# Stick-breaking attention in a hybrid decoder block: differences of V in place of the second sigmoid, the product and the triangular selection

## The chip, the cores and the metric

The kernel runs on one core of a Trainium2 chip. Its time is the device time of one execution in microseconds; smaller is better. The core has five engines that run side by side, each with its own queue of instructions worked off in order: PE (matrix products and transposes), DVE (vector), ACT (scalar, activations), POOL (GpSimd) and SP, which here only issues transfers. Engines wait for each other by semaphores. SBUF is the working memory with 128 partitions, PSUM the small memory into which PE writes.

## The reference

One decoder layer on 1040 tokens (16 learned ones and 1024 real ones) of width 1024. The part that matters here is attention with 16 heads of width 64:

```python
# A[t,s] = sigmoid(z_ts) * prod_{s<j<t} (1 - sigmoid(z_tj)), s < t
z = jnp.einsum("bqhd,bkhd->bhqk", qb, kb) * scale
causal = s_idx < t_idx
log_beta = jax.nn.log_sigmoid(z)
log_fail = jnp.where(causal, log_beta - z, 0.0)
survive = lax.cumsum(log_fail, axis=3, reverse=True) - log_fail
a = jnp.where(causal, jnp.exp(log_beta + survive), 0.0)
o = jnp.einsum("bhqk,bkhd->bqhd", a, vb)
```

Beside attention stand a gated short convolution on the same normalised input, two gates, an output projection, and a gated feed-forward part with a second convolution. Everything is float32; the kernel splits each operand of a large product into a high and a low part and makes two or three products of them.

## The kernel before, in words

The first 940 us are one mixed stage. PE works through a list of 128-column blocks of the input projection (`items`, lines 400 to 416): for each pair of heads p the items of V, Q and K, three of the convolution, and one to four gates. Each item has three chunks of 342 columns and in each chunk eight steps of three products (lines 129 to 131, tile `mm`). Between these steps attention is woven in, unit by unit. A unit is one head and one third of the queries, that is three blocks of 114 queries (`QB`).

- `stage1` (line 316) makes, for each block of queries and each chunk of keys, the products z (lines 330, 331), and on ACT sigmoid(-z) into `fl` (line 332) and sigmoid(z) into `be` (line 333). A deferred step `weights` then runs on DVE a scan over the keys from right to left (line 340). It multiplies up `fl` and takes the maximum with `upper`, which is 1 in the triangle at and above the diagonal, so that the running product starts at 1 there. POOL multiplies `be` by the scan shifted by one key (line 346, in pieces) and zeroes the triangle (line 348). `be` is then A.
- `stage2` (line 358) transposes A in blocks of keys on PE (line 377, tile `tp`), ACT and DVE split it into `ah` and `al` (`split`, lines 65 and 66), and PE multiplies by V (lines 367, 368). ACT and DVE gather the result in `ot` (lines 394, 395), and after the last unit of a pair SP writes `ot` to `o_d`.
- `item_v` (line 246) copies V from PSUM into `vt` with ACT (line 253), transposes it in nine blocks of keys on PE (line 263) in three deferred steps, and splits it into `vv`.

All the weights come in by SP, are cast to a high part by ACT (line 110, `whi`) and subtracted by POOL (line 113, `wlo`), two items ahead.

At the start, nine blocks of input rows (`xt`) are loaded, squared and summed by ACT (line 460), scaled by DVE after a square root on ACT (lines 73 to 78, 462, tile `xn`), transposed by PE (line 184) and split into `xnT`. The first products need the first three blocks.

The order in which the instructions are written is not the order in which each engine has them: a scheduler goes through them with its own estimates of durations, picks for each engine what is ready by those, and gives out the buffers of the pools (a `tag` names a set of slots, `bufs` their number). `ps_tp`, the PSUM tiles `tp` for all transposes of this stage, has two. `fl` has two buffers and `be` six; the `xt` blocks of the start use the tag `be` and the `xn` blocks the tag `fl`. The tag `wk` has four, shared by `vt`, the tiles of the convolution, the gates and `ot`.

Of the kernel before, what the change touches and what calls it, by code (L numbers as in the profile page):

```python
# [8 lines left out]
F32 = mybir.dt.float32  # L9
F32R = mybir.dt.float32r  # L10
AF = mybir.ActivationFunctionType
ALU = mybir.AluOpType
# [21 lines left out]
def block_kernel(ctx, tc, x, meta_tokens, g_pre_mix, w_in, channels, w_proj_conv,  # L34
# [177 lines left out]
    CH_C = [(T0 - 2, CH + 2), (T0 + CH, CH), (T0 + 2 * CH, CH)]  # L212
    CH_K = [(0, T0 + CH), (T0 + CH, CH), (T0 + 2 * CH, CH)]

    QH, QL, KK, V = {}, {}, {}, {}

    def item_q(p):
        def evac(ci, a, n, ps):
# [27 lines left out]
    def item_v(p):  # L246
        st = {}

        def evac(ci, a, n, ps):
            if ci == 0:  # L250
                st["vt"] = work.tile([P, NT], F32, name="vt", tag="wk", bufs=4)
            vt = st["vt"]
            nc.scalar.copy(vt[:, a:a + n], ps)
            if ci < 2:
                return
            vv = heads.tile([P, 9, 2, P], F32R, name="vv", tag="vv", bufs=2)
            V[p] = vv

            def tokens(k0, kn, m):
                tp = ps_tp.tile([P, 512], F32, name="tp", tag="tp")  # L260
                for k in range(kn):
                    s0 = KEYS[k0 + k][0]
                    nc.tensor.transpose(tp[:m, k * P:(k + 1) * P], vt[:, s0:s0 + m], ident)
                tv = tp[:m, :kn * P].rearrange("p (k h d) -> p k h d", k=kn, h=2)
                split(vv[:m, k0:k0 + kn, :, 0:64], vv[:m, k0:k0 + kn, :, 64:128], tv)

            dense.defer(1, lambda: tokens(0, 4, P))
            dense.defer(2, lambda: tokens(4, 4, P))
            dense.defer(3, lambda: tokens(8, 1, QB))
        return (col_block(w_in, 40 + p), src_x, CH_K, evac)  # L270
# [45 lines left out]
    def stage1(p, h, g):  # L316
        res = []
        qh, ql, kk = QH[p][h], QL[p][h], KK[p][h]
        for b in range(3 * g, 3 * g + 3):
            nk = P + QB * b  # L320
            q0 = QB * b
            fl = work.tile([P, NT], F32, name="fl", tag="fl")[:QB]
            be = work.tile([P, NT], F32, name="be", tag="be", bufs=6)[:QB]
            nch = -(-nk // 512)
            wch = 2 * (-(-nk // (2 * nch)))
            c0 = 0
            while c0 < nk:
                n = min(wch, nk - c0)
                z = ps_z.tile([P, 512], F32, name="z", tag="z")[:QB, :n]
                nc.tensor.matmul(z, qh[:, q0:q0 + QB], kk[:, c0:c0 + n], start=True, stop=False)  # L330
                nc.tensor.matmul(z, ql[:, q0:q0 + QB], kk[:, c0:c0 + n], start=False, stop=True)  # L331
                nc.scalar.activation(fl[:, c0:c0 + n], z, AF.Sigmoid, scale=-0.125)  # L332
                nc.scalar.activation(be[:, c0:c0 + n], z, AF.Sigmoid, scale=0.125)
                c0 += n
                if late:
                    late.pop(0)()
                if c0 < nk:
                    yield n
            def weights(fl=fl, be=be, nk=nk):
                nc.vector.tensor_tensor_scan(fl[:, :nk][:, ::-1], fl[:, :nk][:, ::-1],  # L340
                                             upper[:, NT - nk:][:, ::-1], 1.0,
                                             op0=ALU.mult, op1=ALU.max)
                w = -(-(nk - 1) // (-(-nk // 384)))
                for a in range(0, nk - 1, w):
                    e = min(a + w, nk - 1)
                    nc.gpsimd.tensor_tensor(be[:, a:e], be[:, a:e], fl[:, a + 1:e + 1],  # L346
                                            op=ALU.mult)
                nc.gpsimd.affine_select(out=be[:, nk - QB:nk], in_=be[:, nk - QB:nk],
                                        pattern=[[-1, QB]], compare_op=ALU.is_gt, fill=0.0,
                                        base=0, channel_multiplier=1)  # L350

            late.append(weights)
            res.append((be, nk))
            if len(res) == 3:
                units[(p, h, g)] = res
            yield n

    def stage2(p, h, g):
        blocks = units.pop((p, h, g))
        vv = V[p]  # L360
        nkb = 3 * g + 3
        av = ps_av.tile([P, 512], F32, name="av", tag="av")[:, :CH]
        pend = []

        def products(kb, n, off, ah, al):
            w = vv[:n, kb, h, :]
            nc.tensor.matmul(av[:, off:], w, ah[:n, off:], start=(kb == 0), stop=False)  # L367
            nc.tensor.matmul(av[:, off:], w, al[:n, off:], start=False, stop=(kb == nkb - 1))  # L368

        unit = COST2[g] / (nkb + 3)  # L370
        for kb in range(nkb):
            k0, n = KEYS[kb]
            js = [j for j in range(3) if blocks[j][1] > k0]
            off = QB * js[0]
            tp = ps_tp.tile([P, 512], F32, name="tp", tag="tp")
            for j in js:
                nc.tensor.transpose(tp[:n, QB * j:QB * (j + 1)], blocks[j][0][:, k0:k0 + n],  # L377
                                    ident[:QB, :QB])
            ah = work.tile([P, CH], F32R, name="ah", tag="ah", bufs=4)
            al = work.tile([P, CH], F32R, name="al", tag="al", bufs=4)  # L380
            split(ah[:n, off:], al[:n, off:], tp[:n, off:CH])
            pend.append((kb, n, off, ah, al))
            if len(pend) > 2:
                products(*pend.pop(0))
            yield unit
        while pend:
            products(*pend.pop(0))
            yield unit
        if (h, g) == (0, 0):
            OT[p] = work.tile([P, NT], F32, name="ot", tag="wk", bufs=4)  # L390
        ot = OT[p]
        a, b = (0, 64) if h == 0 else (64, 0)
        o = ot[a:a + 64, CH * g:CH * (g + 1)]
        nc.scalar.copy(o, av[b:b + 64])
        nc.vector.tensor_tensor(o, av[a:a + 64], o, op=ALU.add)
        if (h, g) == (1, 2):
            nc.sync.dma_start(o_d[p * P:(p + 1) * P, :], ot[:, :NQ])
        yield unit

# [33 lines left out]
    with ExitStack() as p0:  # L433
# [8 lines left out]

        def x_load(b):
            n = P if b < 8 else 16
            xt = work.tile([P, NT], F32, name="xt", tag="be", bufs=6)[:, :D]
            if b == 0:
                nc.sync.dma_start(xt[:NMETA, :], meta_tokens)
                nc.sync.dma_start(xt[NMETA:, :], x[:P - NMETA, :])
            elif b < 9:
                nc.sync.dma_start(xt[:n, :], x[P * b - NMETA:P * b - NMETA + n, :])  # L450
            xts[b] = xt

        def x_block(b):
# [1 line left out]
                x_load(b + 3)  # L455
            n = P if b < 8 else 16
            xt = xts[b]
            xn = work.tile([P, NT], F32, name="xn", tag="fl")[:, :D]
            ssq = small.tile([P, 1], F32, name="ssq", tag="ssq")
            nc.scalar.activation((xn if b < 2 else junk)[:n], xt[:n], AF.Square, accum_out=ssq[:n])  # L460
            r = rstd_of(small, ssq, n)
# [773 lines left out]
```

## Time and profile before

| what | value |
|---|---|
| median of 3 runs | 2027.19 us (2023.95 to 2030.04) |
| the profiled execution | 2019.99 us |
| its span, first to last instruction | 2018.2 us |
| PE busy | 1968.4 us (98%) |
| DVE busy | 1006.3 us (50%) |
| ACT busy | 853.3 us (42%) |
| POOL busy | 1022.7 us (51%) |
| mean granted TensorE clock | 0.993 |

The profile is of one execution. A row of the table of groups has the line, the engine, the operation, the tiles it writes and reads, the shapes and the count; then the busy time in us, the mean of one in ns, and the idle time of the engine just before, with what ended it. A row of the timeline has the start and the length in us. The end of a product on PE is modelled, and products overlap. "PEld" is the load of the stationary operand.

### The profile page before, as it was taken

To read this page: it belongs to the slowest core of one execution; us is meant where nothing else is said; L and a number is where in the kernel's file an instruction comes from. 1 tells how busy PE (TensorE), PEld (TensorE's weight loads), DVE (VectorE), ACT (ScalarE), POOL (GpSimd) and SP (SyncE) were. 2 spreads that over 40 slices of the span, in tenths; PEclk is the share of its full clock that TensorE was granted. 3 is DMA by queue.
4 is the path that set the end of the run, shared out by engine and by line. 5 is a ranking of instruction groups with operands and counts; after the bars stand their busy time and mean duration, and the time that the engine had idled before them with its cause. 6 is when DMAs were issued, how large, how long until landed. Compare 5 with 4: busy or idle time off the path is not lost.

```text
span 2018.2 us, 30990 instructions
## 1 busy us (share of the span) xinstructions
PE 1968.4 (98%) x12228; PEld 1857.0 (92%) x12228; DVE 1006.3 (50%) x1545; ACT 853.3 (42%) x1771; POOL 1022.7 (51%) x1062
## 2 busy tenths in 40 slices
PE   6999999999999999999999999979999999999997
PEld 6999999999999999999999999969988998888886
DVE  6445555555555555553341126874354445345546
ACT  5544555555454545555421123453443344321122
POOL 2643666565555646565223550345556565654353
PEclk9999999999999999999999999989999999999998
DMA  3111101111111111012664673303121212253223
GB/s 137 43 63 43 53 32 64 43 53 43 42 53 43 58 39 62 32 64 73 189 221 156 188 214 114 97 31 126 63 84 67 102 66 82 92 174 111 84 84 136
DMA packets 56174, 177.58 MB, mean 88 GB/s; under 512 B 12872, under 2 KB 12872, under 8 KB 56028
## 3 DMA queue, kind: packets, MB, share of 16 engines
q1 hardware_dynamic: 52704, 165.09, 24.5%
q10 hardware_dynamic: 3324, 10.50, 1.7%
q8 instruction: 96, 1.57, 0.3%
q14 instruction: 50, 0.41, 0.1%
HBM read 131.36 MB, written 44.21 MB: 87 GB/s over the span
## 4 chain that ended last, share of the span: by engine, by line
PE 87%; DVE 7%; ACT 2%; DMA 2%; POOL 1%; issue 1%; ACTq 0%; DVEq 0%; SPq 0%; POOLq 0%
PE mm L129 14%; PE mm L130 14%; PE mm L131 14%; PE st L863 7%; PE st L867 7%; PE st L865 7%; PE tp L377 3%; PE st L1157 3%; PE st L1155 3%; PE st L1156 3%; PE av L368 2%; PE av L367 2%; PE z L331 2%; PE z L330 2%; PE po L706 1%; PE po L708 1%
## 5 line engine op out<-in xcount | busy, mean ns | idle before, releaser
L129 PE MATMUL mm<-xnT,whi 128*128 128x342 f32 (+2 forms) x1536 | 505.5, 329 | 0.3 <-ACT xnT L65 0.2
L130 PE MATMUL mm<-xnT,whi 128*128 128x342 f32 (+2 forms) x1536 | 494.0, 322 | 0.5 <-DVE xnT L66 0.5
L131 PE MATMUL mm<-xnT,wlo 128*128 128x342 f32 (+2 forms) x1536 | 492.3, 320 | 0.0
L346 POOL TENSOR_TENSOR be<-be,fl 114x271 f32<-114x271 f32 (+14 forms) x288 | 206.0, 736 | 310.3 <-DVE fl L340 301.6
L113 POOL TENSOR_TENSOR wlo<-raw,whi 128x256 fp32r<-128x256 f32 x320 | 254.8, 828 | 208.2 <-ACT whi L110 207.3
L130 PEld LDWEIGHTS mm<-xnT,whi 128*128 128x128 f32 x1536 | 291.0, 189 | 2.1 <-DVE xnT L66 1.0
L129 PEld LDWEIGHTS mm<-xnT,whi 128*128 128x128 f32 x1536 | 290.2, 189 | 2.9 <-ACT xnT L65 0.8
L131 PEld LDWEIGHTS mm<-xnT,wlo 128*128 128x128 f32 x1536 | 290.0, 189 | 0.0
L340 DVE TENSOR_TENSOR_SCAN fl<-fl,upper 114x128 f32<-114x128 f32 (+2 forms) x144 | 214.4, 1490 | 112.2 <-ACT fl L332 64.0
L66 POOL TENSOR_TENSOR a_op<-raw,a_op 128x512 fp32r<-128x512 f32 (+1 forms) x136 | 193.7, 1437 | 87.9 <-ACT a_op L65 85.6
L66 DVE TENSOR_TENSOR al<-tp,ah 114x342 fp32r<-114x342 f32 (+3 forms) x288 | 128.3, 452 | 148.8 <-ACT ah L65 147.5
L65 ACT CAST ah<-tp 114x342 fp32r<-114x342 f32 (+3 forms) x288 | 113.0, 398 | 165.3 <-PE tp L377 157.0
L863 PE MATMUL st<-opT,a_op 128*128 128x258 f32 (+2 forms) x528 | 172.3, 326 | 3.2 <-ACT snap L878 1.8
L865 PE MATMUL st<-opT,a_op 128*128 128x258 f32 (+2 forms) x528 | 170.1, 322 | 2.6 <-DVE opT L66 1.7
L867 PE MATMUL st<-opT,a_op 128*128 128x258 f32 (+2 forms) x528 | 170.0, 322 | 0.0
L332 ACT ACTIVATE fl<-z 114x348 f32<-114x348 f32 (+10 forms) x240 | 111.4, 464 | 123.6 <-PE z L331 93.5
L65 ACT CAST a_op<-raw 128x512 fp32r<-128x512 f32 (+1 forms) x136 | 85.1, 634 | 156.0 <-DMA raw<-in_w_up_gate_dram 51.8
L1162 DVE TENSOR_TENSOR acc<-acc,st 128x512 f32<-128x512 f32 x144 | 98.5, 687 | 91.1 <-PE st L1157 91.1
L865 PE MATMUL st<-opB,a_op 128*128 128x512 f32 (+2 forms) x396 | 127.6, 322 | 0.0
L863 PE MATMUL st<-opB,a_op 128*128 128x512 f32 (+2 forms) x396 | 127.6, 322 | 0.0
L867 PE MATMUL st<-opB,a_op 128*128 128x512 f32 (+2 forms) x396 | 127.2, 321 | 0.0
L377 PE MATMUL tp<-ident,be 114*114 114x114 f32 (+1 forms) x720 | 118.5, 262 | 4.1 <-DVE al L66 3.4
(168 smaller groups left out, 4320.5 us busy)
## 6 DMA issues: line engine op xcount, KB each, us to landing
raw<-in_w_in_dram SPq DMA_DIRECT2D x64, 512.0 KB, 3.3
raw<-in_w_up_gate_dram SPq DMA_DIRECT2D x44, 512.0 KB, 3.3
act_d<-owork SPq DMA_DIRECT2D x22, 512.0 KB, 4.3
araw<-act_d SPq DMA_DIRECT2D x22, 512.0 KB
raw<-in_w_down_dram SPq DMA_DIRECT2D x22, 512.0 KB, 3.3
y_d<-yy SPq DMA_DIRECT2D x8, 513.0 KB
ga_d<-gt SPq DMA_DIRECT2D x8, 513.0 KB
o_d<-ot SPq DMA_DIRECT2D x8, 513.0 KB
```

Source lines behind the costliest of these rows:

```text
L65: nc.scalar.copy(hi, src)
L66: (lo_engine or nc.vector).tensor_tensor(lo, src, hi.bitcast(F32), op=ALU.subtract)
L113: nc.gpsimd.tensor_tensor(lo[:, c], raw[:, c], hi[:, c].bitcast(F32), op=ALU.subtract)
L129: nc.tensor.matmul(ps, wh, xh, start=(kb == 0), stop=False)
L130: nc.tensor.matmul(ps, wh, xl, start=False, stop=False)
L131: nc.tensor.matmul(ps, wl, xh, start=False, stop=(kb == KB - 1))
L340: nc.vector.tensor_tensor_scan(fl[:, :nk][:, ::-1], fl[:, :nk][:, ::-1], upper[:, NT - nk:][:, ::-1], 1.0, op0=ALU.mult, op1=ALU.max)
L346: nc.gpsimd.tensor_tensor(be[:, a:e], be[:, a:e], fl[:, a + 1:e + 1], op=ALU.mult)
L377: nc.tensor.transpose(tp[:n, QB * j:QB * (j + 1)], blocks[j][0][:, k0:k0 + n], ident[:QB, :QB])
L863: nc.tensor.matmul(ps, wt[:, 0, k], xh, start=start and kb == 0, stop=False, skip_group_check=True)
L865: nc.tensor.matmul(ps, wt[:, 0, k], xl, start=False, stop=False, skip_group_check=True)
L867: nc.tensor.matmul(ps, wt[:, 1, k], xh, start=False, stop=stop and kb == 3, skip_group_check=True)
```

## The change

With S[t,s] for the running product of sigmoid(-z) over the keys from s to the diagonal, A[t,s] is S[t,s+1] - S[t,s]. Summed by parts, the output is the sum over s of S[t,s] (v[s-1] - v[s]), with v[-1] = 0, plus v of the last key of the block. S is 1 above the diagonal, and these terms cancel down to the right key. So the scan's result `fl` itself is transposed and multiplied, and `be` with its sigmoid, its product and its selection is gone. In its place:

- `item_v` takes the last value of each block of queries into `ve` (POOL), makes `dv`, the differences along the tokens (DVE, one instruction over 1039 columns; the first column on ACT), and transposes `dv` instead of `vt`. `dv` is a further tile of the tag `wk`.
- after the last unit of a pair POOL adds `ve` to `ot`, and the write to `o_d` follows that.
- the tags `fl` (2) and `be` (6) become one tag `fl` with 7, which `xt` and `xn` of the start share.

```diff
             V[p] = vv
+            ends = VE[p] = heads.tile([P, 9], F32, name="ve", tag="ve", bufs=2)
+            nc.gpsimd.tensor_copy(ends, vt[:, P - 1:NT:QB])
+            dv = work.tile([P, NT], F32, name="dv", tag="wk", bufs=4)
+            nc.vector.tensor_tensor(dv[:, 1:], vt[:, :NT - 1], vt[:, 1:], op=ALU.subtract)
+            nc.scalar.mul(dv[:, 0:1], vt[:, 0:1], -1.0)
...
-                    nc.tensor.transpose(tp[:m, k * P:(k + 1) * P], vt[:, s0:s0 + m], ident)
+                    nc.tensor.transpose(tp[:m, k * P:(k + 1) * P], dv[:, s0:s0 + m], ident)
...
-            fl = work.tile([P, NT], F32, name="fl", tag="fl")[:QB]
-            be = work.tile([P, NT], F32, name="be", tag="be", bufs=6)[:QB]
+            fl = work.tile([P, NT], F32, name="fl", tag="fl", bufs=7)[:QB, :nk]
...
-                nc.scalar.activation(be[:, c0:c0 + n], z, AF.Sigmoid, scale=0.125)
...
-                w = -(-(nk - 1) // (-(-nk // 384)))
-                for a in range(0, nk - 1, w):
-                    e = min(a + w, nk - 1)
-                    nc.gpsimd.tensor_tensor(be[:, a:e], be[:, a:e], fl[:, a + 1:e + 1],
-                                            op=ALU.mult)
-                nc.gpsimd.affine_select(out=be[:, nk - QB:nk], in_=be[:, nk - QB:nk],
-                                        pattern=[[-1, QB]], compare_op=ALU.is_gt, fill=0.0,
-                                        base=0, channel_multiplier=1)
...
-            res.append((be, nk))
+            res.append((fl, nk))
...
         if (h, g) == (1, 2):
+            ov = ot[:, :NQ].rearrange("p (b n) -> p b n", n=QB)
+            nc.gpsimd.tensor_tensor(ov, ov, VE[p].unsqueeze(2).to_broadcast([P, 9, QB]), op=ALU.add)
             nc.sync.dma_start(o_d[p * P:(p + 1) * P, :], ot[:, :NQ])
...
-            xt = work.tile([P, NT], F32, name="xt", tag="be", bufs=6)[:, :D]
+            xt = work.tile([P, NT], F32, name="xt", tag="fl", bufs=7)[:, :D]
...
-            xn = work.tile([P, NT], F32, name="xn", tag="fl")[:, :D]
+            xn = work.tile([P, NT], F32, name="xn", tag="fl", bufs=7)[:, :D]
```

The change also moves instructions, since the scheduler makes the order. The first place is the start of ACT's queue. `whi_241` is the cast of the first weight block, `xn_127` and `xn_156` are the squares of input blocks 0 and 1, `junk` those of later ones, `s` a square root. Before:

```order
L460 ACTIVATE xn_127,ssq_128<-xt_112 128x1024
L74 ACTIVATE s_131<-v_130 128x1
L460 ACTIVATE xn_156,ssq_157<-xt_116 128x1024
L74 ACTIVATE s_160<-v_159 128x1
L65 CAST xnT_92<-tp_140 128x4x128
L460 ACTIVATE junk_108,ssq_186<-xt_118 128x1024
L65 CAST xnT_92<-tp_147 128x4x128
L110 CAST whi_241<-raw_120 128x1024
```

The same place in the changed kernel (`s_189` is the root of block 2, `ssq_287` the square of block 4):

```order
L110 CAST whi_241<-raw_120 128x1024
L456 ACTIVATE xn_127,ssq_128<-xt_112 128x1024
L456 ACTIVATE xn_156,ssq_157<-xt_116 128x1024
L74 ACTIVATE s_131<-v_130 128x1
L456 ACTIVATE junk_108,ssq_186<-xt_118 128x1024
L74 ACTIVATE s_160<-v_159 128x1
L110 CAST whi_248<-raw_122 128x1024
L456 ACTIVATE junk_108,ssq_215<-xt_125 128x1024
L74 ACTIVATE s_189<-v_188 128x1
L456 ACTIVATE junk_108,ssq_287<-xt_154 128x1024
L65 CAST xnT_92<-tp_140 128x4x128
```

The first weight cast moved from behind the squares of blocks 0 to 2 to the head of the queue, and the squares moved together ahead of the first cast of a transposed block.

The second place is DVE's queue a little later in the start. `xn_156` and `xn_185` are the scaling of blocks 1 and 2, `xnT<-tp_140` and `tp_147` the subtractions that free the PSUM slots of block 0, which block 1's transposes use next. Before:

```order
L66 TENSOR_TENSOR xnT_92<-tp_140,xnT_92 128x4x128
L462 SCALAR_TENSOR_TENSOR xn_156<-xt_116,s_160,gb_107 128x1024
L66 TENSOR_TENSOR xnT_92<-tp_147,xnT_92 128x4x128
L73 TENSOR_SCALAR v_188<-ssq_186 128x1
L66 TENSOR_TENSOR xnT_92<-tp_169,xnT_92 128x4x128
```

The changed kernel:

```order
L458 SCALAR_TENSOR_TENSOR xn_156<-xt_116,s_160,gb_107 128x1024
L75 RECIPROCAL s_189<-s_189 128x1
L73 TENSOR_SCALAR v_217<-ssq_215 128x1
L76 SCALAR_TENSOR_TENSOR t_190<-s_189,v_188 128x1
L77 TENSOR_SCALAR t_190<-t_190 128x1
L73 TENSOR_SCALAR v_289<-ssq_287 128x1
L78 TENSOR_TENSOR s_189<-s_189,t_190 128x1
L458 SCALAR_TENSOR_TENSOR xn_185<-xt_118,s_189,gb_107 128x1024
L66 TENSOR_TENSOR xnT_92<-tp_140,xnT_92 128x4x128
L66 TENSOR_TENSOR xnT_92<-tp_147,xnT_92 128x4x128
```

The two subtractions of block 0 moved behind the scaling of block 2, and a small step on the square of block 4 (`v_289`) moved ahead of that scaling.

The third place is DVE's queue where V of pair 2 is finished; the other pairs from 1 on have the like. `fl` are scans of 470, 584 and 698 keys, `vv` the low parts of V's transposed blocks, `al` the first low part of the next unit of `stage2`. Before:

```order
L340 SCALAR_TENSOR_TENSOR fl_2755<-fl_2755,upper_93 114x470
L66 TENSOR_TENSOR vv_2792<-tp_2793,vv_2792 128x8x64
L340 SCALAR_TENSOR_TENSOR fl_2774<-fl_2774,upper_93 114x584
L66 TENSOR_TENSOR vv_2792<-tp_2818,vv_2792 128x8x64
L66 TENSOR_TENSOR vv_2792<-tp_2828,vv_2792 114x2x64
L340 SCALAR_TENSOR_TENSOR fl_2832<-fl_2832,upper_93 114x698
L66 TENSOR_TENSOR al_2866<-tp_2861,ah_2865 128x342
```

The changed kernel:

```order
L343 SCALAR_TENSOR_TENSOR fl_2603<-fl_2603,upper_93 114x470
L261 TENSOR_TENSOR dv_2634<-vt_2512 128x1039
L343 SCALAR_TENSOR_TENSOR fl_2618<-fl_2618,upper_93 114x584
L66 TENSOR_TENSOR vv_2631<-tp_2637,vv_2631 128x8x64
L66 TENSOR_TENSOR vv_2631<-tp_2661,vv_2631 128x8x64
L343 SCALAR_TENSOR_TENSOR fl_2675<-fl_2675,upper_93 114x698
L66 TENSOR_TENSOR vv_2631<-tp_2671,vv_2631 114x2x64
L66 TENSOR_TENSOR al_2703<-tp_2698,ah_2702 128x342
```

The difference `dv` is new ahead of the scan of 584, and every `vv` moved one place back. On PE, the transposes of V stood right behind V's last product; in the changed kernel they stand here (`mm_2657` is already the item of Q, `z_2687` a z product):

```order
L131 MATMUL mm_2657<-xnT_92,wlo_2442 128x342
L334 MATMUL z_2687<-kk_1683,qh_1551 114x348
L268 MATMUL tp_2637<-ident_61,dv_2634 128x128 x4
L268 MATMUL tp_2661<-ident_61,dv_2634 128x128 x4
L335 MATMUL z_2687<-kk_1683,ql_1553 114x348
```

Between V's last product and these eight transposes there are now 17 products of z and of Q, and the ninth block follows six products later.

More of the change, by code (lines that the diff above doesn't have):

```diff
@@ L213, in block_kernel @@
     CH_K = [(0, T0 + CH), (T0 + CH, CH), (T0 + 2 * CH, CH)]
-    QH, QL, KK, V = {}, {}, {}, {}
+    QH, QL, KK, V, VE = {}, {}, {}, {}, {}
     def item_q(p):
@@ L338, in stage1, with weights @@
                     yield n
-            def weights(fl=fl, be=be, nk=nk):
-                nc.vector.tensor_tensor_scan(fl[:, :nk][:, ::-1], fl[:, :nk][:, ::-1],
-                                             upper[:, NT - nk:][:, ::-1], 1.0,
+            def weights(fl=fl, nk=nk):
+                nc.vector.tensor_tensor_scan(fl[:, ::-1], fl[:, ::-1], upper[:, NT - nk:][:, ::-1], 1.0,
                                              op0=ALU.mult, op1=ALU.max)
-                w = -(-(nk - 1) // (-(-nk // 384)))
-                for a in range(0, nk - 1, w):
-                    e = min(a + w, nk - 1)
-                    nc.gpsimd.tensor_tensor(be[:, a:e], be[:, a:e], fl[:, a + 1:e + 1],
-                                            op=ALU.mult)
-                nc.gpsimd.affine_select(out=be[:, nk - QB:nk], in_=be[:, nk - QB:nk],
-                                        pattern=[[-1, QB]], compare_op=ALU.is_gt, fill=0.0,
-                                        base=0, channel_multiplier=1)
             late.append(weights)
-            res.append((be, nk))
+            res.append((fl, nk))
             if len(res) == 3:
```

## The prediction

> **What bounds the kernel now.** I read the page's busy shares first, then the busy time by stage (windows: stretch, length, busy time and instructions of PE, PEld, DVE, ACT, POOL, then clock and DMA).
>
> ```profile
> PE 1968.4 (98%) x12228; PEld 1857.0 (92%) x12228; DVE 1006.3 (50%) x1545; ACT 853.3 (42%) x1771; POOL 1022.7 (51%) x1062
> 0.00:20.54 20.54, 5.64 (x24) 4.70 (x24) 10.22 (x26) 12.13 (x22) 11.18 (x19) 1.00 0.85 307
> 20.54:60.00 39.46, 38.02 (x240) 36.14 (x240) 26.40 (x65) 19.33 (x43) 5.65 (x8) 1.00 0.13 43
> 60.00:940.00 880.00, 874.55 (x5780) 855.32 (x5780) 472.56 (x678) 457.35 (x1044) 505.23 (x660) 1.00 0.14 49
> 940.00:2018.00 1078.00, 1050.20 (x6189) 960.85 (x6187) 497.12 (x778) 364.50 (x662) 500.64 (x376) 0.99 0.36 118
> ```
>
> Attention runs from about 60 to 940 us. PE is busy for 874.55 of those 880 us, so 5.45 us is all that a faster DVE, ACT or POOL could hand back there. The other place within reach of this change is the start: PE works 5.64 of the first 20.54 us. From the last attention unit on, the built order of PE is the same in both kernels, so I leave the last 1078 us as they are. The table of waits says what PE waits for (total, times, longest):
>
> ```profile
> PE tp L184 <- DVE xn L462: 14.9, 3, 9.1
> PE tp L377 <- DVE al L66: 3.4, 5, 2.1
> PE z L330 <- ACT be L333: 1.3, 1, 1.3
> ```
>
> The first row is the start. The other two are attention, 4.7 us together.
>
> **What goes.** The table of groups gives busy time and mean ns of one:
>
> ```profile
> L346 POOL TENSOR_TENSOR be<-be,fl 114x271 f32<-114x271 f32 (+14 forms) x288 | 206.0, 736 | 310.3 <-DVE fl L340 301.6
> L348 POOL TENSOR_SCALAR_AFFINE_SELECT be<-be 114x114 f32<-114x114 f32 x144 | 113.6, 789 | 10.1
> L333 ACT ACTIVATE be<-z 114x348 f32<-114x348 f32 (+10 forms) x240 | 110.6, 461 | 0.0
> ```
>
> POOL loses 206.0 + 113.6 = 319.6 us of work and ACT 110.6 us. Neither is what PE stands still for, so of all this only the 4.7 us can come back. The z wait shortens by the 0.46 us of the second sigmoid, which no longer holds z's bank. The L377 waits end on a DVE subtraction queued behind scans, and the scans stay; only where the scan itself was held up by POOL do they go. I take 2.0 us back, with 0 and 4.7 as ends. PE itself keeps 12,228 products.
>
> **Small additions.** On POOL, the add on `ot` has 1026 columns; at L346's 736 ns for 271 that is 2.8 us, eight times. It delays the write of `o_d` by that, and SP's weight loads and POOL's weight subtractions behind it. The slot that `ot` frees is next written by a gate:
>
> ```profile
> 199.57 0.33 SPq L397 DMA_DIRECT2D o_d<-ot  x1
> 225.80 0.55 ACT L304 ACTIVATE gt<-mm,par 128x342 f32<-128x342 f32 x1
> ```
>
> There are 26 us between, and weights are loaded two items ahead, so I cost it at nothing; uncovered it would be 8 x 2.8 = 22 us. The copies of `ve` and the one-column product on ACT are a few tenths of a us, eight times, beside other work.
>
> **The start.** The shared tag `fl` makes the scheduler write ACT's queue in another order: the cast of the first weight block now stands ahead of the first square. SP issues x0 (512 KB), the gain, x1, x2 and then that block, so it is the fifth 512 KB, and ACT now waits for it. Rows of the DMA view (GB/s in 1.5 us slices) and of the timeline:
>
> ```profile
> GB/s 0 137 317 257 393 407 431 404 399 407 347 126 382 227 292 77 0 0 0 16 5 0 0 0 0 0 0 0 0 0 0 0 0 0 11 0 238 112 90 259
> 5.22 1.06 ACT L460 ACTIVATE xn<-xt 128x1024 f32<-128x1024 f32 x1 [2.92 <-DMA xt<-in_x_dram]
> 6.59 0.20 ACT L74 ACTIVATE s<-v 128x1 f32<-128x1 f32 x1 [0.22 <-DVE v L73]
> 7.66 1.28 DVE L462 SCALAR_TENSOR_TENSOR xn<-xt,s,gb 128x1024 f32<-128x1024 f32 x1
> 8.34 1.06 ACT L460 ACTIVATE xn<-xt 128x1024 f32<-128x1024 f32 x1 [1.55 <-DMA xt<-in_x_dram]
> 9.09 1.94 PE L184 MATMUL tp<-ident,xn 128*128 128x128 f32 x8 [9.09 <-DVE xn L462]
> 14.60 0.69 DVE L66 TENSOR_TENSOR xnT<-tp,xnT 128x512 fp32r<-128x512 f32 x1 [1.22 <-ACT xnT L65]
> 15.98 1.07 ACT L460 ACTIVATE junk<-xt 128x1024 f32<-128x1024 f32 x1
> 17.17 1.06 ACT L460 ACTIVATE junk<-xt 128x1024 f32<-128x1024 f32 x1
> 18.78 1.94 PE L184 MATMUL tp<-ident,xn 128*128 128x128 f32 x8 [3.98 <-DVE xn L462]
> 20.54 0.95 PE L129 MATMUL mm<-xnT,whi 128*128 128x356 f32 x2
> 34.55 0.66 PE L184 MATMUL tp<-ident,xn 128*128 128x128 f32 x4 [0.67 <-DVE xnT L66]
> ```
>
> Summing the slices, x1's last byte (1.57 MB) is in at 7.3 us and its square starts at 8.34, 1.0 later. The weight block ends at 2.62 MB, 9.8 us, so ACT can cast it at 10.8. I then walk ACT's new queue: cast to 11.9 (1.05), squares of x0 and x1 (1.19 apart, rows 15.98 and 17.17) to 14.3, root 0.2, square of x2 to 15.7, root, second weight cast to 16.95, square of x3, root at 18.15, square of x4 to 19.55. DVE scales x0 1.07 after its root (rows 6.59, 7.66): 15.4 to 16.7. About 1.0 of small steps later it scales x1, 17.7 to 19.0. One small step ahead of x2 now needs the sum of x4 (19.55), so x2 is scaled from 20.1 to 21.4. Only behind that stand the two subtractions of block 0 (0.69 each), to 22.1 and 22.8. PE's transposes of block 1 need the bank that they free: they run from 22.1 to 24.1 (1.94) instead of from 12.87. ACT casts them; DVE does eight small steps (1.6, to 24.4), then their subtractions, to 25.1 and 25.8. Block 2's transposes end at 27.1, and the first product starts there instead of at 20.54: **6.6 us later**. PE is full afterwards, and what it could regain is a wait like the one of 0.67 at 34.55. The ends: 5.0 (that wait regained, and the weight usable 1.0 sooner, as soon as its bytes are in) and 7.8 (two scalings slowed by 0.6 each beside POOL, the gap between 1218 and 1835 in the rows below). On SP, x5's load falls behind a weight load that waits for POOL to finish the first block, about 15.3; its square comes at 21, so that is covered.
>
> **The differences of V.** Until now PE transposes four blocks of V as soon as its second third is copied. Now everything waits for the last third, then for a subtraction of 128x1039 on DVE. No such row exists; two of 128x1032 bound it:
>
> ```profile
> L775 DVE TENSOR_TENSOR opT<-xr,opT 128x1032 fp32r<-128x1032 f32 x1 | 1.2, 1218 | 0.0
> L775 DVE TENSOR_TENSOR xr<-xr 128x1032 f32<-128x1032 f32 x4 | 7.3, 1835 | 0.0
> L66 DVE TENSOR_TENSOR al<-tp,ah 128x342 fp32r<-128x342 f32 x48 | 24.2, 504 | 16.7 <-ACT ah L65 16.4
> 254.23 0.32 PE L131 MATMUL mm<-xnT,wlo 128*128 128x342 f32 x1
> 254.43 1.05 ACT L110 CAST whi<-raw 128x1024 fp32r<-128x1024 f32 x1
> 255.38 0.44 ACT L253 COPY vt<-mm 128x342 f32<-128x342 f32 x1
> 255.56 3.97 POOL L113 TENSOR_TENSOR wlo<-raw,whi 128x256 fp32r<-128x256 f32 x4
> 256.33 0.69 DVE L66 TENSOR_TENSOR vv<-tp,vv 128x512 fp32r<-128x512 f32 x1 [2.59 <-ACT vv L65]
> 256.94 1.37 DVE L340 TENSOR_TENSOR_SCAN fl<-fl,upper 114x584 f32<-114x584 f32 x1
> 258.22 0.86 DVE L66 TENSOR_TENSOR vv<-tp,vv 128x512 fp32r<-128x512 f32 x2
> 259.10 1.91 DVE L340 TENSOR_TENSOR_SCAN fl<-fl,upper 114x698 f32<-114x698 f32 x1
> 261.46 0.31 PE L377 MATMUL tp<-ident,be 114*114 114x114 f32 x1
> ```
>
> I count from V's last product, 254.23. The copy ends 1.6 later (a weight cast stands ahead of it in ACT's queue, before and after). The difference ends at 2.8 to 3.45. PE comes to the transposes 17 products later, 17 x 0.16 = 2.7, so it waits 0.1 to 0.7 at once. What counts more is that DVE's queue was already what PE waits for here. New chain on DVE: scan of 584 (1.37), to 4.2 or 4.8; two of `vv` (0.69 each), 5.6 or 6.2; scan of 698 (1.64 in proportion, or the 1.91 seen), 7.2 or 8.1; the short `vv` (0.2 to 0.3), 7.45 or 8.35; `al` (0.50), 7.95 or 8.85. The transposes that need its slot ran at 7.23 before (261.46), behind one product (0.16) less: PE comes 0.6 to 1.5 us late, say 1.0. Pair 0's V is covered by the 24 products of Q that follow it; pairs 1 to 7 make **7.0 us**, with ends 4 and 10.5.
>
> The Trainium skill (SBUF — State Buffer, Who interferes with whom) says that a DVE instruction with two SBUF inputs and a GpSimd instruction that reads SBUF lock each other out for a whole instruction. By that, the difference would wait for the running weight subtraction and then take its 1.2, close to the 1835 row; the sum would have about 1.4 instead of 1.0 per pair, 9.8 instead of 7.0. No run here shows the difference yet.
>
> **Sum.** 6.6 + 7.0 - 2.0 = 11.6 us. The profiled execution took 2019.99 (its span of 2018.2 and 1.8 around it), so it would be 2031.6. The median of the runs, 2027.19, lies 7.2 above that execution; I add the same difference: **2038.8**.
>
> **Rivals.** (a) Only the start is paid: the V chain is swallowed by waits that PE has anyway. Against it: PE has 0.5 us idle per 100 us there. 6.6 - 2.0 gives 2031.8.
>
> (b) No change: PE's products are the same, and the start is regained as later blocks are squared earlier. For it: idle time of an engine off the path costs nothing. Against it: the one start wait left to regain is 0.67. 2027.2. The skill (Perfetto Trace Analysis, Identifying the Most-Contended Engine) has the same rule: work on the engine with the highest occupancy first, and that is PE, untouched here.
>
> (c) Faster: PE's busy time hides waits, since its ends are modelled.
>
> ```profile
> L129 PE MATMUL mm<-xnT,whi 128*128 128x342 f32 (+2 forms) x1536 | 505.5, 329 | 0.3 <-ACT xnT L65 0.2
> L131 PE MATMUL mm<-xnT,wlo 128*128 128x342 f32 (+2 forms) x1536 | 492.3, 320 | 0.0
> ```
>
> If the 9 ns more of each L129 were waits for evacuations that ACT now does sooner, 1536 x 9 ns = 13.8 us go, and with the 4.7 and the start that makes -11.9: 2015.3. It decides from 13 us of hidden waits on. Against it: L129 is the product that mostly follows transposes and z, and the switch itself may be the 9 ns; and the two waits that the table does name for attention are 4.7 us.
>
> (d) Much slower: the difference and both scans each wait for a whole weight subtraction (3.97 / 4 = 1.0), 3.0 on top of the 0.6: 7 x 3.6 + 6.6 - 2.0 = 29.8, 2057.
>
> **Chances.** Forecast 0.64, (a) 0.16, (b) 0.08, (c) 0.06, (d) 0.06. The forecast's own ends are 5.0 + 4 - 4.7 = 4.3 and 7.8 + 10.5 = 18.3, that is 2031.5 to 2045.5. The range 2027 to 2047 takes in (a) and half of (b). A measurement of this kernel tells 0.3%, 6.1 us, from no change. Slower by more: 0.58 of the forecast, (d), and 0.02 of (a), 0.66. Within: the rest of these and (b), 0.28. Faster: (c), 0.06.
>
> **What would show it.** In the changed kernel's profile: ACT's first row a cast near 10.8 us, PE's first product near 27; at each pair's V a wait of PE on the new transposes or on `al` behind a late scan, 0.6 to 1.5 us; POOL and ACT lower by some 300 and 110 us. A first product before 24 us, or no added PE wait at the V places, makes the prediction wrong. PE's idle time in attention below 3 us would point to (c).

## The result and the profile after

The changed kernel takes 2043.58 us (median of 6 runs, 2037.76 to 2045.92) beside 2027.37 us of the kernel before on the same chip; the ratio is 1.0075 with a 95% interval of 1.0058 to 1.0092. It is slower by 16 us. Its profiled execution took 2041.25 us with a span of 2039.5 us, 21.3 us more than the span before.

The page of the changed kernel, busy time of each engine, answers to the first line quoted before the change:

```profile
PE 1972.6 (97%) x12228; PEld 1856.0 (91%) x12228; DVE 1012.5 (50%) x1553; ACT 773.8 (38%) x1539; POOL 749.0 (37%) x646
```

POOL lost 274 us of work and ACT 80 us, and PE has as many products as before. POOL lost less than the 319.6 us of the two rows that go, because the add on `ot` (15.3 us) and the copies of `ve` (8.0) came in and its 320 weight subtractions got longer, 893 ns in the mean instead of 828. Now by stage, with the same columns as before:

```profile
0.00:27.73 27.73, 5.80 (x24) 4.57 (x25) 12.15 (x34) 14.21 (x28) 11.41 (x19) 1.00 0.71 242
60.00:940.00 880.00, 867.66 (x5714) 845.48 (x5713) 471.20 (x686) 374.87 (x806) 232.76 (x251) 1.00 0.14 48
```

PE now starts its products at 27.73 us instead of 20.54, and between 60 and 940 us it stands for 12.34 us instead of 5.45. The waits of PE (total, times, longest) name the places:

```profile
PE tp L184 <- DVE v L73: 17.5, 1, 17.5
PE tp L184 <- DVE xnT L66: 5.3, 4, 3.9
PE tp L371 <- DVE al L66: 3.6, 9, 2.0
PE tp L268 <- DVE dv L261: 3.5, 7, 1.2
PE tp L371 <- DVE vv L66: 3.3, 6, 0.6
PE mm L129 <- DVE gal L611: 2.1, 1, 2.1
```

The first two rows are the start. `dv` and `vv` are new: PE waits for `dv` seven times, once per pair from pair 1 on, and for `vv` six times. `al` was 3.4 and is 3.6. `gal` is a gate block of the later projections.

The start on the timeline of the changed kernel:

```profile
11.64 1.04 ACT L110 CAST whi<-raw 128x1024 fp32r<-128x1024 f32 x1 [9.40 <-DMA raw<-in_w_in_dram]
12.59 1.05 ACT L456 ACTIVATE xn<-xt 128x1024 f32<-128x1024 f32 x1
17.46 1.94 PE L184 MATMUL tp<-ident,xn 128*128 128x128 f32 x8 [17.46 <-DVE v L73]
18.64 1.72 DVE L458 SCALAR_TENSOR_TENSOR xn<-xt,s,gb 128x1024 f32<-128x1024 f32 x1
22.58 1.28 DVE L66 TENSOR_TENSOR xnT<-tp,xnT 128x512 fp32r<-128x512 f32 x2
23.32 1.97 PE L184 MATMUL tp<-ident,xn 128*128 128x128 f32 x8 [3.91 <-DVE xnT L66]
27.73 0.59 PE L129 MATMUL mm<-xnT,whi 128*128 128x356 f32 x2
```

ACT's first work is the weight cast, which starts after ACT has stood idle for 9.40 us for its load; everything of the input stands behind it. And V of pair 2, the place shown for the kernel before:

```profile
261.58 1.05 ACT L110 CAST whi<-raw 128x1024 fp32r<-128x1024 f32 x1 [0.41 <-PE mm L130]
262.53 0.44 ACT L253 COPY vt<-mm 128x342 f32<-128x342 f32 x1
262.70 2.42 POOL L113 TENSOR_TENSOR wlo<-raw,whi 128x256 fp32r<-128x256 f32 x2 [14.48 <-ACT whi L110]
263.00 1.54 DVE L261 TENSOR_TENSOR dv<-vt 128x1039 f32<-128x1039 f32 x1 [2.21 <-ACT vt L253]
264.46 1.89 DVE L343 TENSOR_TENSOR_SCAN fl<-fl,upper 114x584 f32<-114x584 f32 x1
264.68 1.07 PE L268 MATMUL tp<-ident,dv 128*128 128x128 f32 x8 [0.39 <-DVE dv L261]
266.28 1.26 DVE L66 TENSOR_TENSOR vv<-tp,vv 128x512 fp32r<-128x512 f32 x2
267.46 1.75 DVE L343 TENSOR_TENSOR_SCAN fl<-fl,upper 114x698 f32<-114x698 f32 x1
269.13 0.26 DVE L66 TENSOR_TENSOR vv<-tp,vv 114x128 fp32r<-114x128 f32 x1
269.44 0.41 PE L371 MATMUL tp<-ident,fl 114*114 114x114 f32 x2 [0.55 <-DVE vv L66]
```

PE waits for `dv` at once (0.39), and again (0.55) for the short `vv`, which stands in DVE's queue behind the scan of 698.

To compare kernels I use one event near the end of attention, the write of a gate block by SP, first in the kernel before and then in the changed one:

```profile
950.72 0.33 SPq L306 DMA_DIRECT2D gc_d<-gt  x1
```

```profile
967.55 0.33 SPq L311 DMA_DIRECT2D gc_d<-gt  x1
```

Of the 21.3 us, 16.8 are lost by then. The other 4.5 us are lost behind attention, where the order of the instructions is the same.

### The profile page after: what moved, and what is told of

It is laid out like the page before. It is cut to its first block, busy times and chain, and to the rows that moved or that the text cites. A ratio compares the mean times of both kernels' runs of the same rounds, so it can differ in the third digit from the quotient of the medians.

```text
span 2039.5 us, 30244 instructions
## 1 busy us (share of the span) xinstructions
PE 1972.6 (97%) x12228; PEld 1856.0 (91%) x12228; DVE 1012.5 (50%) x1553; ACT 773.8 (38%) x1539; POOL 749.0 (37%) x646
## 4 chain that ended last, share of the span: by engine, by line
PE 78%; DVE 10%; DMA 4%; ACT 4%; POOL 2%; issue 2%; SPq 0%; ACTq 0%; DVEq 0%; POOLq 0%
PE mm L129 12%; PE mm L130 12%; PE mm L131 12%; PE st L859 6%; PE st L863 6%; PE st L861 6%; PE st L1151 3%; PE st L1153 3%; PE st L1152 3%; PE tp L371 3%; PE av L362 2%; PE av L361 2%; PE z L335 2%; PE z L334 2%; DVE fl L343 1%
## 5 line engine op out<-in xcount | busy, mean ns | idle before, releaser
L113 POOL TENSOR_TENSOR wlo<-raw,whi 128x256 fp32r<-128x256 f32 x320 | 276.1, 893 | 752.3 <-ACT whi L110 741.1
L343 DVE TENSOR_TENSOR_SCAN fl<-fl,upper 114x128 f32<-114x128 f32 (+2 forms) x144 | 206.6, 1437 | 109.6 <-ACT fl L336 109.1
L110 ACT CAST whi<-raw 128x1024 fp32r<-128x1024 f32 x80 | 83.9, 1049 | 115.0 <-PE mm L131 74.5
L371 PE MATMUL tp<-ident,fl 114*114 114x114 f32 (+1 forms) x720 | 119.4, 263 | 7.3 <-DVE al L66 3.6
```

Source lines behind the costliest of these rows:

```text
L113: nc.gpsimd.tensor_tensor(lo[:, c], raw[:, c], hi[:, c].bitcast(F32), op=ALU.subtract)
L343: nc.vector.tensor_tensor_scan(fl[:, ::-1], fl[:, ::-1], upper[:, NT - nk:][:, ::-1], 1.0, op0=ALU.mult, op1=ALU.max)
```

## The experiments

Theory A says that the start and V are two separate prices, 5.7 us and about 1.2 us per pair, as the trace after shows them. All ratios are to the kernel before on the same chip. "Write" is the event above, its distance from 950.72 behind it; "gate" is PE's longest single wait for `gal` at the last projections (1.3 before, 2.1 after).

| kernel | ratio (95%) | write, us | gate, us |
|---|---|---|---|
| changed | 1.0075 (1.0058 to 1.0092) | 967.55, +16.8 | 2.1 |
| e1 old start | 1.0079 (1.0065 to 1.0093) | 960.87, +10.2 | 6.6 |
| e2 new start alone | 1.0028 (1.0017 to 1.0040) | 956.80, +6.1 | 4.8 |
| e3 no differences | 1.0026 (1.0014 to 1.0039) | 952.18, +1.5 | 5.9 |
| e4 thirds on DVE | 1.0037 (1.0023 to 1.0051) | 954.57, +3.9 | 5.8 |
| e5 before, third gate | 0.9984 (0.9973 to 0.9996) | 950.58, -0.1 | 2.8 |
| e6 changed, third gate | 1.0072 (1.0058 to 1.0086) | 965.24, +14.5 | 2.6 |
| e7 old start, third gate | 1.0044 (1.0027 to 1.0060) | 960.19, +9.5 | 2.4 |
| e8 thirds on POOL, third gate | 1.0035 (1.0022 to 1.0048) | 960.30, +9.6 | 4.9 |
| e9 before again | 0.9992 (0.9980 to 1.0004) | 951.11, +0.4 | 2.5 |
| e10 difference twice | 1.0115 (1.0101 to 1.0130) | 969.69, +19.0 | 6.6 |
| e11 last third on DVE, third gate | 1.0023 (1.0012 to 1.0033) | 951.90, +1.2 | 5.6 |
| e12 weights first | 1.0073 (1.0061 to 1.0085) | 965.69, +15.0 | 6.1 |

### The start: e1, e2, e12

e1 takes the start back and leaves attention as changed:

```diff
-            fl = work.tile([P, NT], F32, name="fl", tag="fl", bufs=7)[:QB, :nk]
+            fl = work.tile([P, NT], F32, name="fl", tag="fl", bufs=6)[:QB, :nk]
...
-            xn = work.tile([P, NT], F32, name="xn", tag="fl", bufs=7)[:, :D]
+            xn = work.tile([P, D], F32, name="xn", tag="xn", bufs=2)
```

(`xt` has 6 buffers too.)

> The changed kernel with the start's tags apart (xn in a tag of its own with 2 buffers, xt and fl share 6): the start's order is that of the kernel before, attention's order that of the changed kernel. Theory A (start and V are two separate prices): first product back at 20.5 us, the gap at the second item 0 instead of 5.7, and the same 1.2 us per pair in attention; time 5.7 us under the changed kernel, about 2037.5, ratio to before 1.005. Rival B (the late start moves all that follows, the losses at V are its consequence): the V waits go too, time within 3 us of the kernel before.

The first product is back at 20.44 us, and PE waits for `dv` and `vv` as long as before it, 3.5 and 3.3 us:

```profile
PE tp L268 <- DVE dv L261: 3.5, 7, 1.2
PE tp L371 <- DVE vv L66: 3.3, 6, 0.6
```

At the write it is 6.7 us ahead of the changed kernel (960.87 against 967.55). So the V waits don't hang on the late start, and rival B falls. Yet the ratio, 1.0079, is no better than the changed kernel's: theory A has its size in the trace and misses the time. Of the 6.7 us, 5.6 are the start: matched product by product, the changed kernel is 5.6 us behind e1 at 100 us. At 120 us it is 7.0 behind, because PE had a lower clock for some microseconds in the changed kernel and not in e1 (last section). The 6.6 us at the gate show where e1's profiled run lost part of its lead; the third group below takes that up.

e2 gives the kernel before the new start and nothing else:

```diff
-            fl = work.tile([P, NT], F32, name="fl", tag="fl")[:QB]
-            be = work.tile([P, NT], F32, name="be", tag="be", bufs=6)[:QB]
+            fl = work.tile([P, NT], F32, name="fl", tag="fl", bufs=8)[:QB]
+            be = work.tile([P, NT], F32, name="be", tag="fl", bufs=8)[:QB]
```

(`xt` and `xn` share the tag too.)

> The kernel before with xt, xn, fl and be in one tag with 8 buffers: it gets the start order of the changed kernel, and its attention stays. Theory A: first product at 27.7 us, 5.7 us behind from the second item on and no more after that: before + 5.7, ratio 1.0028. Rival (start regained in attention's waits): back within 2 us by 100 us, ratio below 1.001.

```profile
10.87 1.04 ACT L110 CAST whi<-raw 128x1024 fp32r<-128x1024 f32 x1 [8.57 <-DMA raw<-in_w_in_dram]
27.34 0.95 PE L129 MATMUL mm<-xnT,whi 128*128 128x356 f32 x2 [0.29 <-ACT xnT L65]
```

First product at 27.34, 6.1 us behind at the write, ratio 1.0028, which is 5.7 us: the start costs what theory A says, with the old attention. Matched product by product, e2 is 6.3 us behind at 60 us and 6.1 at the write, so hardly any of it is regained.

e12 loads the first two weight blocks sooner; ACT's queue still begins with the first cast:

```diff
         nc.sync.dma_start(gb, g_pre_mix.partition_broadcast(P))
-        x_load(1)
-        x_load(2)
         dense.load(0)
         dense.load(1)
+        x_load(1)
+        x_load(2)
```

> The changed kernel with the loads of the first two weight blocks issued ahead of input blocks 1 and 2. ACT's queue still begins with the cast. Theory A (the start is late because this cast waits for the fifth load): the cast starts at about 8.3 us instead of 11.6, PE's first transposes at about 14.3 instead of 17.5, first product near 24.5 instead of 27.7; 2 to 3 us under the changed kernel up to 1183 us. Rival F (the input blocks, now later, set the first product as before): first product 27 or later.

```profile
8.60 1.04 ACT L110 CAST whi<-raw 128x1024 fp32r<-128x1024 f32 x1 [6.37 <-DMA raw<-in_w_in_dram]
15.85 1.94 PE L184 MATMUL tp<-ident,xn 128*128 128x128 f32 x8 [15.85 <-DVE v L73]
24.38 0.95 PE L129 MATMUL mm<-xnT,whi 128*128 128x356 f32 x2
```

The cast came 3.0 us sooner and the first product 3.35 us sooner, so the later input blocks don't hold the start at 27 us or more, and rival F falls. But e12 changes more than the time of the load, since the scheduler wrote the queues anew. The second weight cast now stands ahead of the squares too (at 9.87 us), and PE's first transposes come only 1.6 us sooner. DVE's subtractions of block 0 stand ahead of the scaling of block 2 again, and the transposes of block 1 come at 18.82 us instead of 23.32. How much of the late start is the wait for the load, and how much DVE's order, no run separates. At the write 1.9 us of the gain were left. The ratio of 1.0073 can't tell 2 us from none.

### The differences of V: e3, e4, e8, e10, e11

All five have e1's start. e3 takes the differences out and transposes `vt`, so that its output is not the layer's:

```diff
-            dv = work.tile([P, NT], F32, name="dv", tag="wk", bufs=4)
-            nc.vector.tensor_tensor(dv[:, 1:], vt[:, :NT - 1], vt[:, 1:], op=ALU.subtract)
-            nc.scalar.mul(dv[:, 0:1], vt[:, 0:1], -1.0)
...
-                    nc.tensor.transpose(tp[:m, k * P:(k + 1) * P], dv[:, s0:s0 + m], ident)
+                    nc.tensor.transpose(tp[:m, k * P:(k + 1) * P], vt[:, s0:s0 + m], ident)
```

> As e1, but without the differences: V itself is transposed and multiplied, so the output lacks the summation by parts; the sigmoid, product and selection stay away and the add of the last value stays. Theory A: V's transposes stand right behind V's last product as before, no step of 0.9 us at V, attention as in the kernel before less the waits given back: 0 to 4.7 us under the kernel before (2.0 forecast), ratio 0.999. Rival C (hidden waits of PE on ACT and POOL): 10 us or more under the kernel before, ratio 0.995 or less.

At the write it is 8.7 us ahead of e1 (952.18 against 960.87): that is the price of the differences, 1.2 us for each of seven pairs. But it is not ahead of the kernel before. Rival C falls: with 283 us less on POOL and 81 less on ACT the kernel is not faster: 1.5 us behind at the write, ratio 1.0026. The part of theory A on waits given back falls as well. The waits of PE in e3:

```profile
PE tp L368 <- DVE al L66: 3.9, 10, 2.0
PE z L331 <- ACT fl L333: 1.0, 1, 1.0
```

The z wait fell from 1.3 to 1.0, and that on `al` grew from 3.4 to 3.9. Matched product by product, the two traces show a new loss of 0.27 us in each pair from 1 on, where DVE works the convolution. First the kernel before, then e3, the same place:

```profile
319.06 1.29 DVE L203 SCALAR_TENSOR_TENSOR yy<-cc,par,yy 128x1026 f32<-128x1026 f32 x1 [1.47 <-ACT yy L202]
320.26 0.51 DVE L66 TENSOR_TENSOR al<-tp,ah 128x342 fp32r<-128x342 f32 x1
320.84 0.32 PE L129 MATMUL mm<-xnT,whi 128*128 128x342 f32 x1
321.00 0.27 PE L377 MATMUL tp<-ident,be 114*114 114x114 f32 x1
```

```profile
318.27 1.45 DVE L203 SCALAR_TENSOR_TENSOR yy<-cc,par,yy 128x1026 f32<-128x1026 f32 x1 [1.57 <-ACT yy L202]
319.64 0.50 DVE L66 TENSOR_TENSOR al<-tp,ah 128x342 fp32r<-128x342 f32 x1
319.81 0.32 PE L129 MATMUL mm<-xnT,whi 128*128 128x342 f32 x1
320.20 0.13 PEld L368 LDWEIGHTS tp<-ident,fl 114*114 114x114 f32 x1 [0.35 <-DVE al L66]
```

The first convolution step lasts 1.45 us instead of 1.29, in every pair from 1 on. The `al` behind it in DVE's queue, which frees the slot for the transpose, ends at 320.14, and the transpose comes at 320.20, 0.39 us behind the product before it (PE's weight load waited 0.35 for `al`). In the kernel before it came 0.16 behind that product. POOL's weight subtraction runs beside this step in both kernels; that it now meets the step at another point is a possible reason, which no run isolates. e11 below has the same loss of 0.25 us per pair; e2, with the old attention, has none.

e4 makes `dv` in three pieces:

```diff
             nc.scalar.copy(vt[:, a:a + n], ps)
+            if ci == 0:
+                nc.scalar.mul(dv[:, 0:1], vt[:, 0:1], -1.0)
+            a0 = max(a, 1)
+            nc.vector.tensor_tensor(dv[:, a0:a + n], vt[:, a0 - 1:a + n - 1], vt[:, a0:a + n],
+                                    op=ALU.subtract)
```

> As e1, but dv is made in three pieces on DVE, each as soon as its third of V is copied; only the last piece (about 0.6 us) lies behind V's last product. Theory A (the lateness of one long difference in DVE's queue is the price): PE waits on dv under 0.2 us per pair, the step per pair falls from 1.2 to 0.3 or less, time within 2 us of the kernel before, ratio 0.999 to 1.001. Rival D (1.5 us more of DVE work per pair is paid wherever it stands): the step stays near 1.2, ratio 1.004 to 1.005.

```profile
PE tp L271 <- DVE dv L258: 2.6, 7, 0.9
```

The `vv` wait is gone and 6.3 of the 8.7 us are back (954.57). PE still waits 0.37 us per pair for the last piece, more than the 0.2 expected. The work of `dv` on DVE is not less (14.7 us in all against 12.2), so rival D falls: where the work stands counts here, not how much it is. The ratio of 1.0037 is still over theory A's 0.999 to 1.001, with 5.8 us at the gate.

e8 gives the three pieces to POOL, which has 63% of its time free: `nc.gpsimd.tensor_tensor` in e4's line, and the third gate buffer of e5.

> As e7, but dv is made in three pieces on POOL (about 1.2 us each at the 893 ns of its 256-column subtraction), each as soon as its third of V is copied. Theory A: DVE's queue at V is that of e3, PE waits on dv up to 0.9 us per pair, the step per pair is 0.3 to 0.9; 2 to 5 us over e5, ratio to before 0.998. Rival D2 (POOL's piece waits behind a weight subtraction, or slows DVE beside it): the step per pair 1.2 as with one long difference, ratio 1.002.

```profile
PE tp L271 <- POOL dv L258: 9.8, 7, 2.0
```

Rival D2 is right here: PE waits 1.4 us per pair, and the write comes at 960.30, as with one long difference. A piece takes 0.83 us on POOL (0.61 on DVE in e4), and at V of pair 2 the last one starts at 258.04 us, only when two weight subtractions in POOL's queue (1.42 us) are done, 1.1 us after its columns are copied. A half-idle engine is no help at this place if its queue is taken at that moment.

e10 makes the difference twice, by repeating the subtraction of 1039 columns.

> As e1, but the difference is made twice, one after the other into the same tile: 1.52 us more on DVE per pair at the same place. Theory A (DVE's queue is what PE waits for at V): 1.0 to 1.5 us more per pair, 7 to 10.6 us over e1 up to 968 us, ratio to before about 1.012. Rival E (PE waits only for the transposes of V to begin, and has other products to put there): under 3 us more, ratio 1.009 or less.

```profile
PE tp L269 <- DVE dv L262: 10.6, 8, 1.5
```

It loses 8.8 us more than e1 by the write (969.69 against 960.87), 1.26 us per pair for a second `dv` of 1.27 us (mean). At this place nearly all that is put into DVE's queue is paid by PE. Rival E falls.

e11 also takes the copy of the last third of V off ACT, where it stands behind the weight cast:

```diff
-            nc.scalar.copy(vt[:, a:a + n], ps)
+            (nc.vector.tensor_copy if ci == 2 else nc.scalar.copy)(vt[:, a:a + n], ps)
```

with the third gate buffer.

> As e4 (dv in three pieces on DVE, old start), with the copy of the last third of V on DVE too, which no longer stands behind the weight cast in ACT's queue, and with the third gate buffer. Theory A: the last piece is ready 0.5 to 1 us earlier, PE waits on dv under 1 us in all instead of 2.6, loss up to 968 us 1.5 to 2.5 instead of 3.9; ratio to before 0.999 to 1.0. Rival: the copy's 0.5 us on DVE costs what it saves, 3.9 or more.

No wait for `dv` is left among PE's, and the write comes at 951.90, 1.2 us behind the kernel before and 0.3 ahead of e3. With the weight cast out of the chain the differences cost nothing up to the write. (The third gate buffer is a second change against e4; between e1 and e7 it moves the write by 0.7 us.) The ratio is 1.0023, over the expected 1.0: still slower, with 5.6 us at the gate in the profiled run.

### What is lost behind attention: e5, e6, e7, e9

e5 is the kernel before with three buffers for gates (`bufs=3` for `gal`, `gcl` and the late `gt`).

> The kernel before with a third buffer for the gates of the projections, so that each gate block is loaded one item earlier and PE no longer stands for the last one (1.3 us in the profile before, 4.8 to 6.8 in e1, e2, e3 and e4, plus a slow start after it). Theory G (the 6.5 us between the median and the profiled run of before are this wait): 5 to 8 us under the kernel before, ratio 0.996 to 0.9975. Rival (they lie elsewhere): within 2 us of the kernel before, ratio 0.999 or more.

The ratio is 0.9984, 3 us, less than theory G wants, and the wait is there, 2.8 us. e9 is the kernel before once more.

> The kernel before once more, unchanged. Theory G (its profiled run was a lucky one at the gates): the profile now shows a wait on the last gate of 3 us or more instead of 1.3 and, up to 1183 us, the same times within 0.5; the ratio to itself shows what a measurement can tell, 0.9985 to 1.0015. Rival: 1.3 again, and the 6.5 us between median and profile lie in stages before or after.

Up to 1183 us its products stand within 0.8 us of the first profile; the gate wait is 2.5 us. Its profiled run is again below its median, and the wait doesn't account for that. Theory G falls in both. e9 also says what a ratio is worth here: 0.9980 to 1.0004 for the same kernel, so that e5's 0.9984 can hardly be told from no change.

Why the third buffer doesn't help is in the traces: the wait for `gal` doesn't end on the load of a gate. The load of the last block of `w_out` (tile `w_o`), first in the kernel before:

```profile
1179.72 0.33 SPq L640 DMA_DIRECT2D raw<-in_w_out_dram  x1
1182.92 1.05 ACT L65 CAST w_o<-raw 128x1024 fp32r<-128x1024 f32 x1 [4.55 <-DMA raw<-in_w_out_dram]
```

and in e1, with the chain behind it:

```profile
1192.83 0.33 SPq L636 DMA_DIRECT2D raw<-in_w_out_dram  x1
1200.21 1.05 ACT L65 CAST w_o<-raw 128x1024 fp32r<-128x1024 f32 x1 [8.74 <-DMA raw<-in_w_out_dram]
1201.33 2.17 POOL L66 TENSOR_TENSOR w_o<-raw,w_o 128x1024 fp32r<-128x1024 f32 x1 [3.99 <-ACT w_o L65]
1203.46 0.90 POOL L612 TENSOR_TENSOR gal<-gal,ml 128x342 f32<-128x342 f32 x1
1204.72 0.47 DVE L66 TENSOR_TENSOR mb<-gal,mb 128x114 fp32r<-128x114 f32 x2 [12.13 <-ACT mb L65]
1205.10 1.52 DVE L611 TENSOR_TENSOR gal<-gal,mm 128x342 f32<-128x342 f32 x3
```

ACT casts this block when it is in, POOL subtracts, POOL's add on `gal` stands behind that in its queue, ACT and DVE split the sum into `mb`, and only then does DVE come to the `gal` for which PE waits. From issue to cast it is 3.2 us in the kernel before and 7.4 in e1. The same holds in all the kernels: 3.2 to 3.9 us where the gate wait is 1.3 to 2.8 (before, changed, e5, e6, e7, e9), and 5.8 to 7.4 where it is 4.8 to 6.6 (e1, e2, e3, e4, e8, e10, e11, e12). Why this load took so much longer in some profiled runs stays open.

e6 and e7 are the changed kernel and e1 with three gate buffers.

> The changed kernel with the third gate buffer. Its loss up to 1183 us (18.0) is left, and the wait at the gates goes: by theory G about 18 over e5, near 2038, ratio to before 1.0055. Rival: still 1.0075.

> e1 with the third gate buffer. Theory G with A: what e1 gained at the start (6.5 of 18.0 us up to 1183) and lost again at the gates now reaches the end: 6 us under e6, 11.5 over e5, ratio to before 1.002. Rival (the end absorbs the start whatever the gates do): within 2 us of e6.

e6 has the ratio that its rival expects: the third buffer gives the changed kernel nothing. Between e6 and e7 the start's gain reaches the end: e7 is 5.1 us ahead at the write (960.19 against 965.24) and 7.6 us in the medians (2034.19 against 2041.79); the intervals of the two ratios just touch. So theory A holds where the gates lie alike (2.6 and 2.4 us), and the rival of e7 falls. For e1 its profiled run shows where most of the lead went: between 1183 and 1300 us, matched product by product, it loses 7.3 us against the kernel before, and the changed kernel 2.3. Whether its timed runs met the slow load as well no trace says, so it stays open why they don't show the 6.7 us.

## Why the prediction was right, and where not

The median came out 4.8 us above the forecast of 2038.8 and inside the range; the sign and the mechanism were right, three steps were not. That the number came so close is partly luck: the profiled execution lost 21.3 us where 11.6 were forecast, 9.7 too few, and the 7.2 us added from profile to median were 4.9 too many.

- **What bounds the kernel.** Right. e3 has 283 us less on POOL and 81 less on ACT, and PE gains nothing.
- **The start, forecast 6.6.** Right. Cast at 11.64 for 10.8, block 1's transposes at 23.32 for 22.1, first product at 27.73 for 27.1. The first product is 7.2 us late, and by 60 us 5.7 are left. e2 measures 5.7 by the ratio and 6.1 at the write, e1 5.6 at 100 us. That the wait for the load and DVE's order do this together fits the rows, but no run takes them apart. A slow scaling, which was part of the upper end, came once (1.72 us at 18.64).
- **The differences, forecast 7.0.** The mechanism was right, the size is 8.7 (e1 less e3 at the write). `dv` lasts 1.52 us, between the rows of 1.22 and 1.84. The wait at once is 0.50 us per pair (forecast 0.1 to 0.7). The second wait is behind the late scan as forecast, but it is on the short `vv` (0.55), one place ahead of `al`. The Trainium skill (SBUF — State Buffer, Who interferes with whom) would have had `dv` wait for the running weight subtraction: the rows show the subtraction from 262.70 and `dv` from 263.00, side by side, 1.21 us for each of the two subtractions and 1.54 for `dv`. So the wait for a whole instruction isn't seen. Both are longer than elsewhere: e10's second `dv` took 1.27 in the mean, and the mean of the weight subtractions is 0.89.
- **Waits back, forecast -2.0.** Wrong, and this is the step that failed: the term is +1.5 (e3 at the write), 3.5 us off. "The L377 waits end on a DVE subtraction queued behind scans, and the scans stay" was right, and they stayed at 3.6; to give 2.0 back all the same was not argued from a row. Of the 4.7, only 0.3 of the z wait came back, and the place of the convolution step lost 0.27 per pair, which the forecast had not seen.
- **The add on `ot`, forecast nothing.** Right: 1.91 us each for the 2.8 reckoned, and PE's table of waits names no wait on it; whether the later write of `o_d` has a part in the 1.1 us of the next point, no run shows. The copy of `ve` took 1.01 us each instead of a few tenths, and is not in that table either.
- **"I leave the last 1078 us as they are."** Wrong by 4.5 us in the profiled runs. The order there is the same, but the time isn't: the waits at the gate end differ between 1.3 and 6.6 us over these kernels, with the load of one weight block. In the changed kernel, 1.1 of the 4.5 us are lost by 1026 us, where PE waits for gates that stand in ACT's queue behind casts held by their loads, and 2.3 between 1183 and 1300 us, with a gate wait of 2.1 us and a lower clock behind it.
- **The 7.2 us added from profile to median.** It didn't carry over: the changed kernel's profiled run lies 2.3 below its median. This pulls the other way than the two steps before it: the trace lost 21.3 us and the medians 16.

Of the rivals, (a) fell to e1 and e3 (the rows give PE 0.6 us of idle time per 100 us, 5.45 of 880, not the 0.5 held against it), (b) to e2, (c) to e3; (d) would have needed 3.6 us per pair where 1.2 were measured.

## What to carry to other kernels

When one engine is 98% busy, ask of every instruction that a change adds in which queue it stands between two instructions of that engine; 1.5 us on a half-idle DVE cost 1.2 us each time, and the same work in pieces, most of it ahead of the last chunk and without the cast in front, cost nothing up to the end of attention. A change of buffer tags can reorder the start of a kernel whose scheduler gives out buffers; look at the first ten rows of each queue for an instruction that now waits for a later load. And give no wait back on a list of hopes: take back only those whose releaser is the work that goes. Follow a wait through the queues to its end before choosing a remedy: the one put down to `gal` on DVE ended on a weight load several steps further back, and a buffer for gates could not shorten it.

## What the runs showed of the hardware

The same stand of PE can be followed by a slow stretch or not. `al` of pair 0 holds PE for 2.11 us in the kernel before and 2.02 us in the changed one; the windows around it (granted clock is the third column from the end), first before:

```profile
102.00:106.00 4.00, 1.89 (x14) 1.74 (x14) 3.54 (x6) 0.45 (x1) 3.94 (x5) 1.00 0.39 131
106.00:110.00 4.00, 4.00 (x30) 3.96 (x28) 1.70 (x4) 1.05 (x3) 0.28 (x1) 1.00 0.00 0
```

```profile
108.00:112.00 4.00, 2.61 (x11) 2.61 (x12) 2.69 (x5) 0.45 (x1) 0.72 (x1) 0.68 0.38 131
112.00:116.00 4.00, 4.00 (x26) 3.89 (x26) 1.42 (x3) 0.91 (x3) 0.00 (x0) 0.89 0.00 0
```

In the changed kernel the clock fell to 0.68 and PE did 26 products in the next 4 us instead of 30. Matched product by product, this put it 1.4 us further behind e1, whose clock stayed at 1.00 behind a stand of 2.01 us. The same at the gates: 2.1 us (changed), 2.5 (e9) and 2.8 (e5) were followed by a lower clock, 2.4 (e7) and 2.6 (e6) were not, and all waits of 4.8 us and more were. In e1, behind 6.6 us, it was 0.50 from 1203 to 1208 us. The Trainium skill (TensorE: Matmul & The Clock Gate, Part 1) says that the clock halves after an idle window of about 3.4 us that runs freely. The long waits agree, and here a stand of 2.0 us was enough at times, so the measurement goes further than the page.
